# A hybrid decoder layer on one core: the whole up projection in 512-column products, its convolution taps moved from VectorE to ScalarE copies and adding DMAs

## The chip, the cores and the metric

The kernel runs on one core of a Trainium2 chip, in one launch. The metric is the device time of one execution in microseconds (us), the median of several runs. Engines are named as in the profile: PE is TensorE (PEld its weight loads), DVE is VectorE, ACT is ScalarE, POOL is GpSimd and SP is SyncE; POOL and SP issue the DMAs here.

## The reference, cut to what matters

One layer: a token mixer, a layer norm, a gated feed-forward part with a short convolution, and a second layer norm. Everything is float32, SEQ is 512, D_MODEL is 2048 and D_FF is 5632.

```python
def _causal_conv3(x, w):
    xp = jnp.pad(x, ((0, 0), (2, 0), (0, 0)))
    return w[0] * xp[:, :-2] + w[1] * xp[:, 1:-1] + w[2] * xp[:, 2:]

def _conv_ffn(h, w_up, conv_w, conv_b, w_down):
    up = _causal_conv3(h @ w_up, conv_w) + conv_b
    a, g = jnp.split(up, 2, axis=-1)
    return (jax.nn.silu(g) * a) @ w_down

def reference(x, w_in, conv_mix_w, w_out, ln1_g, ln1_b, w_up, ffn_conv_w, ffn_conv_b,
              w_down, ln2_g, ln2_b, rel_bias):
    for layer in range(DEPTH):
        mix = _token_mixer(x, w_in[layer], conv_mix_w[layer], w_out[layer], rel_bias)
        x = _layernorm(ALPHA * x + mix, ln1_g[layer], ln1_b[layer])
        ffn = _conv_ffn(x, w_up[layer], ffn_conv_w[layer], ffn_conv_b[layer], w_down[layer])
        x = _layernorm(ALPHA * x + ffn, ln2_g[layer], ln2_b[layer])
    return x
```

## The kernel before, in words

**Stages.** The input projection (48 pairs of 128-column output tiles), attention with the first part of the output projection, the rest of the output projection with the first layer norm, the up projection (FT = 44 pairs, each one value tile and one gate tile of 128 channels by 512 positions), and the down projection with the second norm. In the trace the up projection lies from about 1245 to 2125 us.

**Precision.** Each float32 operand is split into a rounded high part and a remainder. For weights, ACT writes the high part (`whi`, line 217) and DVE the remainder (`wlo`, line 220); a product is high weight by high activation, high weight by low activation, and low weight by high activation.

**Pairs.** A pair of output tiles is computed by Winograd's form of Strassen's scheme: seven products (numbered 1 to 7 in `PROD`) of quarter blocks. The weight side of a product is a raw block (B11, B21, B22) or one of four sums T1 to T4, which DVE forms into a tile `tt` (line 207). The seven results are combined in PSUM banks, with some partial results copied out by ACT (a "snapshot") before the bank is added to further.

**Narrow and wide products.** In `product` (narrow, lines 372, 373, 376) each of the eight high-weight blocks meets the high and the low activation in two matmuls of 256 columns, and eight more matmuls of 256 columns use the low weight: 24 matmuls. In `product_wide` (lines 349, 352) the high and low activation lie side by side, and one matmul of 512 columns takes both: 16 matmuls. A wide result has two halves in its bank, so a wide pair ends in four combines of two DVE instructions each (an add of bank and snapshot, line 430, and an add of the two halves into the output tile `o`, line 1132), where a narrow pair ends in two (line 670). The input projection's full pairs are all wide. In the up projection, pair 0 is "plain" (ordinary block products), pairs 1 to 5 have products 1 and 2 done ahead and five narrow products left (`MAIN` without 1 and 2), and of pairs 6 to 43 every third is wide (`p % every == 0` with `every` 3): 13 wide, 25 narrow.

**Weights.** Blocks of 1 MB come by SP's queue into `RAWS` = 3 buffers, in order; a load waits until the block three before it has been used up by the last `wlo` that reads it. `pump` runs ahead of PE by RING = 4 operands: when PE is done with an operand, the operand four later gets its sum (DVE), its `whi` (ACT), and the operand before that one its `wlo` (DVE). Each engine executes in program order.

**After a pair.** `done3` is called when all of a pair's output `o` is there. ACT writes `cv` = weight[2] * o + bias (line 1115, two instructions); DVE adds the two shifted taps with `taps` (line 696, two instructions for the gate half, two for the value half), ACT applies Silu to the gate half (line 1119), DVE multiplies (line 1122), and POOL sends 256 KB to `act_d` in DRAM (line 1123). `later(n, fn)` puts a step off by n products: the program emits it after the n-th product from then. The last pair's outputs are read back for the down projection.

## Time and profile before

| | before |
|---|---|
| median of 3 runs | 2617.81 us (2616.57 to 2621.77) |
| the profiled execution, its own time | 2619.59 us |
| its span in the trace | 2617.8 us |
| PE busy | 2586.3 us (99% of the span) |
| DVE busy | 2156.1 us (82%) |
| ACT busy | 1205.6 us (46%) |

The span runs from the first to the last instruction of the trace; the execution's own time is 1.8 us more. Busy time counts every moment in which at least one instruction of the engine is recorded as running; since one instruction's record may reach into the next one's, the mean duration of an instruction can be a little longer than the step from one start to the next.

### The profile page before, as it was taken

How to read it: one execution, taken by the hardware profiler on the slowest of the kernel's cores; microseconds unless marked ns; L12 is line 12 of the kernel's file. 1: busy time of each engine (PE TensorE's matmuls, PEld its weight loads, DVE VectorE, ACT ScalarE, POOL GpSimd, SP SyncE). 2: the span in 40 equal slices, each digit the busy share in tenths (PEclk: the TensorE clock that was granted, in tenths of full speed). 3: DMA queues.
4: the chain of work that ended last, by engine and by line, in shares of the span. 5: the costliest groups of instructions: out<-in, count | busy, mean ns of one | idle time of the engine just before them, and what ended most of it. 6: DMA issues, size and time to landing. Idle time of an engine off the chain costs nothing.

```text
span 2617.8 us, 39148 instructions
## 1 busy us (share of the span) xinstructions
PE 2586.3 (99%) x16034; PEld 2329.8 (89%) x16034; DVE 2156.1 (82%) x2575; ACT 1205.6 (46%) x1617; POOL 125.4 (5%) x217
## 2 busy tenths in 40 slices
PE   8999999999999999999999999999999999999997
PEld 8988888888888878888999999999999988888886
DVE  7999888898898876656899999999999965765557
ACT  5444444444544445434655555555555552222220
POOL 0000100000000002221000000000000000000000
PEclk9999999999999999999999999999999999999999
DMA  7423543433433457643443333333333353434331
GB/s 245 168 102 111 188 150 122 145 137 121 145 137 122 144 200 253 244 177 105 167 159 117 128 110 125 116 123 125 109 129 115 120 205 141 153 125 161 113 129 65
DMA packets 70228, 376.34 MB, mean 144 GB/s; under 512 B 9920, under 2 KB 13792, under 8 KB 35360
## 3 DMA queue, kind: packets, MB, share of 16 engines
q1 hardware_dynamic: 51680, 311.47, 34.0%
q0 software_dynamic: 18368, 62.36, 6.5%
q8 instruction: 126, 2.06, 0.3%
q14 instruction: 54, 0.44, 0.1%
HBM read 328.61 MB, written 48.84 MB: 144 GB/s over the span
## 4 chain that ended last, share of the span: by engine, by line
PE 92%; DVE 4%; DMA 2%; ACT 1%; issue 1%; SPq 0%; POOL 0%; DVEq 0%; ACTq 0%
PE bk L349 27%; PE bk L352 14%; PE bk L376 8%; PE bk L373 8%; PE bk L372 8%; PE bk L517 8%; PE bk L519 8%; PE bk L518 8%; DVE wlo L220 1%; DMA raw<-in_w_in_dram 1%; DVE tt L207 1%; DMA ycr<-yc_d 1%; PE bk L851 1%; PE bk L797 0%; PE bk L781 0%
## 5 line engine op out<-in xcount | busy, mean ns | idle before, releaser
L217 ACT ACTIVATE whi<-raw 128x1024 fp32r<-128x1024 f32 x394 | 413.9, 1057 | 521.2 <-PE bk L519 204.1
L220 DVE TENSOR_TENSOR wlo<-raw,whi 128x1024 fp32r<-128x1024 f32 x394 | 480.0, 1221 | 176.7 <-ACT whi L217 175.9
L217 ACT ACTIVATE whi<-tt 128x1024 fp32r<-128x1024 f32 x360 | 380.6, 1057 | 292.4 <-DVE tt L207 167.6
L220 DVE TENSOR_TENSOR wlo<-tt,whi 128x1024 fp32r<-128x1024 f32 x360 | 439.5, 1221 | 39.6 <-ACT whi L217 36.4
L349 PE MATMUL bk<-S,whi 128*128 128x512 f32 x1760 | 440.9, 392 | 0.0
L349 PEld LDWEIGHTS bk<-S,whi 128*128 128x128 f32 x1760 | 316.5, 189 | 56.9 <-ACT s L449 0.4
L349 PE MATMUL bk<-A,whi 128*128 128x512 f32 x1320 | 330.8, 392 | 0.0
L372 PE MATMUL bk<-S,whi 128*128 128x256 f32 x1152 | 283.1, 283 | 0.8 <-ACT z L470 0.8
L373 PE MATMUL bk<-S,whi 128*128 128x256 f32 x1152 | 282.7, 283 | 0.0
L349 PEld LDWEIGHTS bk<-A,whi 128*128 128x128 f32 x1320 | 237.4, 189 | 44.0 <-ACT whi L217 0.9
L352 PEld LDWEIGHTS bk<-S,wlo 128*128 128x128 f32 x1760 | 240.1, 190 | 17.1
L352 PE MATMUL bk<-S,wlo 128*128 128x256 f32 x1760 | 245.4, 282 | 0.0
L372 PE MATMUL bk<-A,whi 128*128 128x256 f32 x936 | 233.5, 286 | 4.0 <-ACT A L312 2.6
L373 PE MATMUL bk<-A,whi 128*128 128x256 f32 x936 | 232.9, 286 | 1.6 <-DVE A L313 1.5
L372 PEld LDWEIGHTS bk<-S,whi 128*128 128x128 f32 x1152 | 221.1, 192 | 1.7 <-ACT z L470 1.7
L373 PEld LDWEIGHTS bk<-S,whi 128*128 128x128 f32 x1152 | 221.2, 192 | 0.0
L207 DVE TENSOR_TENSOR tt<-raw,tt 128x1024 f32<-128x1024 f32 x180 | 219.2, 1218 | 0.0
L352 PEld LDWEIGHTS bk<-A,wlo 128*128 128x128 f32 x1320 | 180.1, 190 | 12.9
L517 PE MATMUL bk<-whi,A 128*128 128x512 f32 x480 | 186.7, 389 | 0.0
L518 PE MATMUL bk<-wlo,A 128*128 128x512 f32 x480 | 186.7, 389 | 0.0
L519 PE MATMUL bk<-whi,A 128*128 128x512 f32 x480 | 186.7, 389 | 0.0
L372 PEld LDWEIGHTS bk<-A,whi 128*128 128x128 f32 x936 | 181.6, 194 | 5.3 <-ACT A L312 3.1
(206 smaller groups left out, 3985.3 us busy)
## 6 DMA issues: line engine op xcount, KB each, us to landing
raw<-in_w_in_dram SPq DMA_DIRECT2D x97, 1024.0 KB, 4.9
raw<-in_w_up_dram SPq DMA_DIRECT2D x89, 1024.0 KB, 5.3
raw<-in_w_down_dram SPq DMA_DIRECT2D x44, 1024.0 KB, 4.9
qkv_d<-o POOLq DMA_DIRECT2D x36, 512.0 KB, 3.9
raw<-in_w_out_dram SPq DMA_DIRECT2D x16, 1024.0 KB, 6.6
act_d<-z POOLq DMA_DIRECT2D x44, 256.0 KB, 5.2
qk<-qkv_d SPq DMA_DIRECT2D x7, 1536.0 KB, 10.3
ar<-act_d SPq DMA_DIRECT2D x9, 1024.0 KB, 6.9
```

Source lines behind the costliest of these rows:

```text
L207: nc.vector.tensor_sub(self.src, v[0], prev)
L217: nc.scalar.activation(self.hi, self.src, AF.Copy)
L220: nc.vector.tensor_sub(self.lo, self.src, self.hi.bitcast(F32))
L349: mm(ps, op.hi[:, w], X[xn].both(k), start=first and k == 0, stop=False, skip_group_check=True)
L352: mm(ps[:, 256:], op.lo[:, w], X[xn][0][:, k], start=False, stop=last and k == 7, skip_group_check=True)
L372: mm(ps, op.hi[:, w], xh[:, k], start=first and k == 0, stop=False, skip_group_check=True)
L373: mm(ps, op.hi[:, w], xl[:, k], start=False, stop=False, skip_group_check=True)
L376: mm(ps, op.lo[:, w], xh[:, k], start=False, stop=last and k == 7, skip_group_check=True)
L517: mm(banks[n], yh[:, tt], op.hi[:, w], start=first and i == 0, stop=False)
L518: mm(banks[n], yh[:, tt], op.lo[:, w], start=False, stop=False)
L519: mm(banks[n], yl[:, tt], op.hi[:, w], start=False, stop=last and i == 1)
L851: nc.tensor.transpose(ps[:, i * P:(i + 1) * P], src[:, n, s:s + P], ident)
```

## The change: what it does

- **All pairs 6 to 43 of the up projection become wide**: `run_pairs` no longer has `every`.
- **The taps leave DVE**, but for the last pair: in `done3`, ACT copies the pair's output `o` times a tap's weight (into a tile `t` for shift 1, into `o` itself for shift 2; two 512-column instructions for each), and POOL issues a DMA that adds the copy, shifted, to `cv` in SBUF (`accum_op=OP.add`, 512 KB each). The steps are spread over the products that follow: `start` one product later, the taps two and three later, the gate (Silu) nine later (`TAPS`) and the multiply with its store ten later.
- **Weight sums in place of raw blocks**: T1 and T2 overwrite B12, T3 overwrites B11 and T4 overwrites B21. The tiles `tt` go, and `RAWS` becomes 4. T4 now reads B12's place too, so that both blocks of a pair are free only after the pair's last operand. The order of products becomes [1, 5, 2, 6, 3, 7, 4] everywhere (that of `LAST` before), in the input projection too; the scratch tiles that came from `tt` come from the output tiles.
- The stage's small tiles are cut otherwise: `z` from 8 buffers to 4, `cv` two and `t` one of four 256-column blocks.

```diff
+TAPS = 9
-RAWS = 3
+RAWS = 4
-MAIN = [1, 5, 6, 3, 7, 4, 2]
-LAST = [1, 5, 2, 6, 3, 7, 4]
+MAIN = [1, 5, 2, 6, 3, 7, 4]
+REST = [5, 6, 3, 7, 4]
...
-                self.src = tt_tile()
-                prev = v[1] if len(v) > 1 else self.box["T1" if self.kind == "T2" else "T2"]
-                nc.vector.tensor_sub(self.src, v[0], prev)
-                self.box[self.kind] = self.src
+                b = self.box
+                if self.kind == "T1":
+                    b["T"] = v[0]
+                    nc.vector.tensor_sub(b["T"], v[0], v[1])
+                elif self.kind == "T2":
+                    nc.vector.tensor_sub(b["T"], v[0], b["T"])
+                else:
+                    nc.vector.tensor_sub(v[0], v[0], b["T"])
+                self.src = b["T"] if self.kind in ("T1", "T2") else v[0]
...
+            if op.kind == "T2" and ops[i - 1].kind == "T1":
+                back_upto(i)
...
-        parts = {"B11": [b11], "B21": [b21], "B22": [b22], "T1": [b12, b11], "T2": [b22], "T3": [b12, b22],
-                 "T4": [b21]}
+        parts = {"B11": [b11], "B21": [b21], "B22": [b22], "T1": [b12, b11], "T2": [b22, b12], "T3": [b11, b12],
+                 "T4": [b21, b12]}
...
-            seqs.append((p, [q for q in (LAST if p == n - 1 else MAIN) if p >= nplain + npre or q > 2], False))
+            seqs.append((p, MAIN if p >= nplain + npre else REST, False))
...
-            if 1 in seq and put_block and p % every == 0:
+            if 1 in seq and put_block:
                 run_wide(p, seq, X, stile, otile, put_block, done, hook)
...
     def done3(j, o):
-        o = o.rearrange("p (f h) t -> p f (h t)", f=2)
-        cv = [stile3() for _ in range(2)]
-        for f in range(2):
-            ft = j + f * FT
-            nc.scalar.activation(cv[f], o[:, f], AF.Identity, bias=fw_t[:, ft, 3:4], scale=fw_t[:, ft, 2:3])
+        def fh(t):
+            return t.rearrange("p (f h) t -> p f (h t)", f=2)
+
+        o, cv, last = fh(o), fh(cvtile()), j == FT - 1
+
+        def start():
+            for f in range(2):
+                ft = j + f * FT
+                nc.scalar.activation(cv[:, f], o[:, f], AF.Identity, bias=fw_t[:, ft, 3:4], scale=fw_t[:, ft, 2:3])
+
+        def tap(sh):
+            t = fh(cvtile("t", 1)) if sh == 1 else o
+            for f in range(2):
+                ft = j + f * FT
+                nc.scalar.activation(t[:, f], o[:, f], AF.Copy, scale=fw_t[:, ft, 2 - sh:3 - sh])
+            nc.gpsimd.dma_start(cv[:, :, sh:], t[:, :, :S - sh], accum_op=OP.add)
 
         def gate():
-            taps(cv[1], o[:, 1], fw_t[:, j + FT])
-            nc.scalar.activation(cv[1], cv[1], AF.Silu)
+            if last:
+                taps(cv[:, 1], o[:, 1], fw_t[:, j + FT])
+            nc.scalar.activation(cv[:, 1], cv[:, 1], AF.Silu)
...
-        later(1, gate)
-        later(2, lambda: taps(cv[0], o[:, 0], fw_t[:, j]))
-        later(3, mul)
+        if last:
+            start()
+            later(1, gate)
+            later(2, mul)
+            return
+        later(1, start)
+        for sh in (1, 2):
+            later(1 + sh, functools.partial(tap, sh))
+        later(TAPS, gate)
+        later(TAPS + 1, mul)
...
-    run_pairs(plan3, X, stile3, otile3, bands, done3, act_first, block3, 3)
+    run_pairs(plan3, X, stile3, otile3, bands, done3, act_first, block3)
```

DVE in the middle of the up projection, before: the end of one wide pair and the beginning of a narrow one (`raw` are weight blocks, `tt` the sums, `z` snapshots and convolution tiles, `o` the output tile, `bk` a bank).

```order
L430 TENSOR_TENSOR z_16735<-bk_2537_16876,z_16735 128x512
L1132 TENSOR_TENSOR o_16848<-z_16735 128x256
L207 TENSOR_TENSOR tt_16967<-raw_16773,tt_16868 128x1024
L220 TENSOR_TENSOR wlo_16932<-tt_16929,whi_16931 128x1024
L696 SCALAR_TENSOR_TENSOR z_16938<-o_16848,fw_t,z_16938 128x511
L696 SCALAR_TENSOR_TENSOR z_16938<-o_16848,fw_t,z_16938 128x510
L220 TENSOR_TENSOR wlo_16970<-tt_16967,whi_16969 128x1024
L696 SCALAR_TENSOR_TENSOR z_16937<-o_16848,fw_t,z_16937 128x511
L696 SCALAR_TENSOR_TENSOR z_16937<-o_16848,fw_t,z_16937 128x510
L220 TENSOR_TENSOR wlo_17004<-raw_16773,whi_17003 128x1024
L1122 TENSOR_TENSOR z_16937<-z_16937,z_16938 128x512
```

DVE at the like place of the change, from the last combine of one pair to the first of the next:

```order
L436 TENSOR_TENSOR z_16311<-bk_2325_16264,z_16311 128x512
L1164 TENSOR_TENSOR o_16218<-z_16311 128x256
L211 TENSOR_TENSOR raw_16027<-raw_16027 128x1024
L224 TENSOR_TENSOR wlo_16308<-raw_16029,whi_16307 128x1024
L211 TENSOR_TENSOR raw_16029<-raw_16029,raw_16027 128x1024
L224 TENSOR_TENSOR wlo_16337<-raw_16027,whi_16336 128x1024
L224 TENSOR_TENSOR wlo_16361<-raw_16029,whi_16360 128x1024
L1147 TENSOR_TENSOR cv_16133<-cv_16133 128x512
L436 TENSOR_TENSOR z_16305<-bk_2338_16342,z_16305 128x512
L1164 TENSOR_TENSOR o_16400<-z_16305 128x256
L207 TENSOR_TENSOR raw_16209<-raw_16209 128x1024
L224 TENSOR_TENSOR wlo_16388<-raw_16209,whi_16387 128x1024
```

The four tap instructions (L696) are gone, the multiply (now L1147) belongs to the pair before the one that has just ended, and each pair has four such combines.

ACT over the same stretch of the change, from the copy for a pair's last combine (L433) over the snapshots (L455), `start` (L1130), the gate (L1142) and the tap copies (L1136) to the next pair's operands (L221):

```order
L433 ACTIVATE z_14855<-bk_2085_14650 128x512
L455 ACTIVATE z_14877<-bk_2118_14860 128x512
L221 ACTIVATE whi_14880<-raw_14571 128x1024
L1130 ACTIVATE cv_14859<-o_14762,fw_t 128x512 x2
L221 ACTIVATE whi_14904<-raw_14573 128x1024
L1142 ACTIVATE cv_14677<-cv_14677 128x512
L1136 ACTIVATE t_14909<-o_14762,fw_t 128x512 x2
L455 ACTIVATE z_14929<-bk_2112_14832 128x512
L221 ACTIVATE whi_14931<-raw_14753 128x1024
L1136 ACTIVATE o_14762<-o_14762,fw_t 128x512 x2
L221 ACTIVATE whi_14964<-raw_14753 128x1024
L221 ACTIVATE whi_14984<-raw_14755 128x1024
```

Before, the same place held the two instructions of line 1115 and one Silu among the seven conversions; four scaled copies have come in, and the gate is that of the pair before (cv_14677, where `start` writes cv_14859).

POOL's queue in the same stretch of the change; before, a pair had one row of it, the store to `act_d`:

```order
L1137 DMA cv_14677<-o_14580 128x2x510
L1137 DMA cv_14859<-t_14909 128x2x511
L1148 DMA act_d<-cv_14677 128x512
L1137 DMA cv_14859<-o_14762 128x2x510
L1137 DMA cv_15041<-t_15091 128x2x511
L1148 DMA act_d<-cv_14859 128x512
```

Between a pair's two adding DMAs now stands the store of the pair before.

## Rows read from the trace of the kernel before

**Rows 1.** The page's first part and the chain of work that ended last, by engine: busy us, share of the span, instructions; then shares of the span.

```profile
PE 2586.3 (99%) x16034; PEld 2329.8 (89%) x16034; DVE 2156.1 (82%) x2575; ACT 1205.6 (46%) x1617; POOL 125.4 (5%) x217
...
PE 92%; DVE 4%; DMA 2%; ACT 1%; issue 1%; SPq 0%; POOL 0%; DVEq 0%; ACTq 0%
```

**Rows 2.** Busy time of each engine (and instructions) in stretches of 100 us; the first two lie in the input projection where all pairs are wide, the others in the up projection. After the engines: TensorE's granted clock, DMA share, GB/s.

```profile
600.00:700.00 100.00, 100.00 (x575) 88.02 (x574) 87.46 (x97) 49.13 (x58) 3.58 (x5) 1.00 0.38 137
700.00:800.00 100.00, 100.00 (x576) 88.02 (x575) 90.12 (x97) 48.73 (x57) 3.57 (x5) 1.00 0.37 132
...
1300.00:1400.00 100.00, 99.15 (x769) 96.00 (x769) 98.91 (x111) 58.20 (x81) 3.25 (x6) 1.00 0.38 132
1400.00:1500.00 100.00, 100.00 (x749) 95.97 (x748) 92.42 (x100) 53.91 (x70) 3.24 (x6) 1.00 0.36 121
```

**Rows 3.** PE's timeline in a narrow pair: start us, us, the low-weight group of eight that ends each product.

```profile
1696.59 1.12 PE L376 MATMUL bk<-S,wlo 128*128 128x256 f32 x8
1699.47 1.12 PE L376 MATMUL bk<-S,wlo 128*128 128x256 f32 x8
1702.35 1.12 PE L376 MATMUL bk<-A,wlo 128*128 128x256 f32 x8
```

**Rows 4.** The same in a wide pair: the 512-column group of eight that begins each product.

```profile
1731.93 2.00 PE L349 MATMUL bk<-S,whi 128*128 128x512 f32 x8
...
1734.73 2.00 PE L349 MATMUL bk<-S,whi 128*128 128x512 f32 x8
...
1737.52 2.00 PE L349 MATMUL bk<-S,whi 128*128 128x512 f32 x8
```

**Rows 5.** Groups by line from 1320 to 2100 us on ACT: form, count, busy us, mean ns of one, idle time before them and what ended it.

```profile
L217 ACT ACTIVATE whi<-tt 128x1024 fp32r<-128x1024 f32 x159 | 167.7, 1055 | 89.8 <-DVE tt L207 61.3 <-PE bk L349 20.9 <-PE bk L373 7.7
...
L1115 ACT ACTIVATE z<-o,fw_t 128x512 f32<-128x512 f32 x80 | 60.6, 805 | 14.0 <-DVE o L1132 11.8 <-DVE o L670 2.2
...
L1119 ACT ACTIVATE z<-z 128x512 f32<-128x512 f32 x40 | 25.3, 633 | 20.9 <-DVE z L696 20.9
L449 ACT ACTIVATE z<-bk 128x512 f32<-128x512 f32 x39 | 23.1, 592 | 37.2 <-PE bk L352 37.2
```

**Rows 6.** DVE's timeline through that wide pair: start us, us.

```profile
1732.33 1.54 DVE L696 SCALAR_TENSOR_TENSOR z<-o,fw_t,z 128x511 f32<-128x511 f32 x2 [0.18 <-ACT z L1115]
1733.78 1.22 DVE L220 TENSOR_TENSOR wlo<-tt,whi 128x1024 fp32r<-128x1024 f32 x1
...
1737.65 0.68 DVE L1122 TENSOR_TENSOR z<-z,z 128x512 f32<-128x512 f32 x1
1738.25 1.22 DVE L207 TENSOR_TENSOR tt<-raw 128x1024 f32<-128x1024 f32 x1
...
1741.59 1.22 DVE L207 TENSOR_TENSOR tt<-raw,tt 128x1024 f32<-128x1024 f32 x1
1742.72 1.22 DVE L220 TENSOR_TENSOR wlo<-tt,whi 128x1024 fp32r<-128x1024 f32 x1
1743.86 0.68 DVE L430 TENSOR_TENSOR z<-bk,z 128x512 f32<-128x512 f32 x1
1744.57 0.43 DVE L1132 TENSOR_TENSOR o<-z 128x256 f32<-128x256 f32 x1
1744.92 1.22 DVE L220 TENSOR_TENSOR wlo<-tt,whi 128x1024 fp32r<-128x1024 f32 x1
```

**Rows 7.** The only copies of ACT with a scale from a tile in this kernel (the mixer's convolution): min/median/max ns, first and last start, form.

```profile
L708 ACT ACTIVATE o<-o,cw_t x8: 707/716/726, 86.8 to 245.1; 128x512 f32<-128x512 f32 x8
```

**Rows 8.** DMA issues by line: tile, queue, count, KB each, median us from issue to landing; and the spread of the stores to `act_d` and of their read-back.

```profile
raw<-in_w_up_dram SPq DMA_DIRECT2D x89, 1024.0 KB, 5.3
act_d<-z POOLq DMA_DIRECT2D x44, 256.0 KB, 5.2
yc_d<-o POOLq DMA_DIRECT2D x4, 512.0 KB, 3.0
ycr<-yc_d POOLq DMA_DIRECT2D x1, 1024.0 KB, 17.1
...
DMA to landing us min/median/max: 2.3/5.2/14.2
```

**Rows 9.** The entry of the up projection: waits from 1200 to 1270 us (us, times, longest); the chain there; a stretch of 20 us behind it.

```profile
ACT whi L217 <- DMA raw<-in_w_up_dram: 2.7, 1, 2.7
...
PE bk L1035 <- ACT S L1039: 1.8, 1, 1.8
...
1245.30 5.03 DMA raw<-in_w_up_dram
1250.42 1.06 ACT whi L217
...
1262.70:1282.70 20.00, 19.93 (x161) 19.73 (x160) 19.35 (x26) 14.81 (x26) 0.00 (x0) 0.95 0.44 158
```

**Rows 10.** The start of the kernel: the chain, and busy time in stretches of 5 us.

```profile
28.22 4.65 DMA raw<-in_w_in_dram
32.98 1.06 ACT whi L217
...
30.00:35.00 5.00, 2.39 (x9) 1.72 (x9) 4.04 (x6) 3.43 (x6) 0.00 (x0) 0.75 0.94 287
35.00:40.00 5.00, 4.86 (x25) 4.67 (x25) 4.50 (x7) 3.45 (x5) 0.00 (x0) 0.57 0.87 299
```

More of the change, by code (lines that the diff above doesn't have):

```diff
@@ L183, in load_next @@
         st["load"] += 1
-    def tt_tile():
-        return wpool.tile([P, UNIT], F32, tag="tt", name=nm("tt"), bufs=3)
     class Op:
@@ L457, in run_wide, with run_pairs @@
                 hook(p, q)
-    def run_pairs(pl, X, stile, otile, bands, done, hook=None, put_block=None, every=1):
+    def run_pairs(pl, X, stile, otile, bands, done, hook=None, put_block=None):
         for p, seq, pre in pl:
@@ L540, in s_alloc, with s_first @@
         X["pools"] = pools
-    def s_first(X, raw, k):
+    def s_first(X, raw, k, scratch):
         ks = slice(k, k + 2)
         a11, a21, a22 = raw["S2"][k // 2][:, 0], raw["S4"][k // 2][:, 0], raw["S4"][k // 2][:, 1]
-        s3 = tt_tile().rearrange("p (s t) -> p s t", t=256)[:, :2]
+        s3 = scratch()[:, :2]
         put(X, "A22", ks, a22)
@@ L582, in layer_kernel, with otile1 @@
     tp = mkpool(tps, "tp1", "right")
+    def otile1():
+        return tp.tile([P, 4, 256], F32, tag="o", name=nm("o"), bufs=3)
     def x_load(i, k):
@@ L589, in x_split @@
         split(X[n][0][:, k:k + 2], X[n][1][:, k:k + 2], raw["S2"][k // 2][:, i])
-    wt = tt_tile()[:, :256 + P]
+    wt = otile1().rearrange("p a t -> p (a t)")[:, :256 + P]
     nc.vector.memset(wt, 0.0)
@@ L624, in layer_kernel @@
         plan_work(XS + i // 2, x_split, 1, 2 * i)
-        plan_work(XF[i], s_first, X, raw, 2 * i)
-        plan_work(XR[i], s_rest, X, raw, 2 * i)
+        plan_work(XF[i], s_first, X, raw, 2 * i, otile1)
+        plan_work(XR[i], s_rest, X, raw, 2 * i, otile1)
     hook = schedule(todo)
@@ L949, in otile3, with cvtile @@
         return chp.tile([P, 4, 256], F32, tag="o", name=nm("o"), bufs=2)
+    def cvtile(tag="cv", bufs=2):
+        return chp.tile([P, 4, 256], F32, tag=tag, name=nm(tag), bufs=bufs)
     def keep3():
@@ L954, in stile3, with ztiles @@
     def stile3(b=None):
-        return zbp.tile([P, 512], F32, tag="z", name=nm("z"), bufs=8)
-    def ztile(t):
-        return stile3() if t >= 2 else zap.tile([P, 512], F32, tag="z", name=nm("z"), bufs=8)
-    z = [[ztile(t) for c in range(4)] for t in range(4)]
+        return zbp.tile([P, 512], F32, tag="z", name=nm("z"), bufs=4)
+    def ztiles(t):
+        if t == 2:
+            return [o.rearrange("p (a b) t -> p a (b t)", a=2)[:, i] for o in (cvtile(), cvtile()) for i in range(2)]
+        return [stile3() if t == 3 else zap.tile([P, 512], F32, tag="z", name=nm("z"), bufs=8) for c in range(4)]
+    z = [ztiles(t) for t in range(4)]
     for c in range(4):
@@ L1076, in layer_kernel @@
         plan_work(HF + 2 * i + 1, tr_k, 2 * i + 1, 1, raw["S4"])
-        plan_work(HF + 2 * i + 1, s_first, X, raw, 2 * i)
-        plan_work(HR[i], s_rest, X, raw, 2 * i)
+        plan_work(HF + 2 * i + 1, s_first, X, raw, 2 * i, otile3)
+        plan_work(HR[i], s_rest, X, raw, 2 * i, otile3)
     hook = schedule(todo)
@@ L1110, in done3 @@
     def done3(j, o):
-        o = o.rearrange("p (f h) t -> p f (h t)", f=2)
-        cv = [stile3() for _ in range(2)]
-        for f in range(2):
-            ft = j + f * FT
-            nc.scalar.activation(cv[f], o[:, f], AF.Identity, bias=fw_t[:, ft, 3:4], scale=fw_t[:, ft, 2:3])
+        def fh(t):
[11 more added lines that the diff above has]
+            nc.gpsimd.dma_start(cv[:, :, sh:], t[:, :, :S - sh], accum_op=OP.add)
         def gate():
-            taps(cv[1], o[:, 1], fw_t[:, j + FT])
-            nc.scalar.activation(cv[1], cv[1], AF.Silu)
+            if last:
+                taps(cv[:, 1], o[:, 1], fw_t[:, j + FT])
+            nc.scalar.activation(cv[:, 1], cv[:, 1], AF.Silu)
         def mul():
-            nc.vector.tensor_mul(cv[0], cv[0], cv[1])
-            nc.gpsimd.dma_start(act_d[:, j, :], cv[0])
-        later(1, gate)
-        later(2, lambda: taps(cv[0], o[:, 0], fw_t[:, j]))
-        later(3, mul)
+            if last:
+                taps(cv[:, 0], o[:, 0], fw_t[:, j])
+            nc.vector.tensor_mul(cv[:, 0], cv[:, 0], cv[:, 1])
+            nc.gpsimd.dma_start(act_d[:, j, :], cv[:, 0])
+        if last:
+            start()
[7 more added lines that the diff above has]
+        later(TAPS + 1, mul)
     run_plain(plan3, X, otile3, done3, hook)
```

7 lines of the change are left out of this document (2 added, 5 removed).

## The prediction, made before the changed kernel had run

> **What bounds the kernel now.** I read the page's first part and its chain first: PE is busy 99% of the span and holds 92% of the chain that ended last [rows 1], so time is saved only where PE gets less to do, or where one of its few stalls goes. The stretches come next: in the up projection PE is at 99 to 100% at a granted clock of 1.00, with DVE at 92 to 99% and ACT at 54 to 58% [rows 2]. So PE sets the pace there and DVE is the engine nearest to taking over. In the stretch at 98.9% DVE, PE was still at 99.15%: the four operands that run ahead of PE hide a DVE that is almost full. Last I read the timelines of a narrow and a wide pair, for the step from one product to the next.
>
> **What PE saves.** The low-weight groups of a narrow pair start at 1696.59, 1699.47 and 1702.35, 2.88 us apart [rows 3]. The 512-column groups of a wide pair start at 1731.93, 1734.73 and 1737.52, on average 2.795 apart [rows 4]. Both forms stream the same columns; the wide one has eight instructions fewer. The change turns 25 pairs of seven products from narrow to wide: 175 products by 0.085 us are 14.9 us. Pair 0, the five pairs with five products each and the products done ahead stay narrow, and the input projection was wide already; their new order alone moves nothing on PE. The clock is at 1.00 on both sides.
>
> **What DVE pays and gets back.** Of a wide pair the starts [rows 6] give 1.14 us for a 1024-column instruction (1741.59, 1742.72, 1743.86), 1.06 for a combine of two (1743.86 to 1744.92), 1.45 for two taps (1732.33 to 1733.78) and 0.60 for the multiply (1737.65 to 1738.25). A pair has seven remainders and four sums, eleven by 1.14, or 12.5 us; with four combines, 4.2, and the multiply, 0.6, that is 17.4. PE needs 7 x 2.795 = 19.57. With its taps a wide pair takes 20.3, more than PE: now every third pair overruns and the narrow ones between make it good. Without taps all of them fit, with 2.2 us to spare. Sums written in place are as many and as long as before. The input projection is a trial of such a load: wide pairs, DVE 87 to 90%, PE 100% [rows 2].
>
> **What ACT takes on.** Per pair: seven conversions at 1.06, four bank copies at 0.59, `start` at 2 x 0.76, a Silu of 0.63 [rows 5], and four scaled copies at 0.72 [rows 7]: 7.4 + 2.4 + 1.5 + 0.6 + 2.9 = 14.8 of 19.57 us, so ACT has room on average. But they come bunched. From the end of the sum T4 on, ACT's order is the rest of `start` (about 0.1), whi of T4, Silu, two copies, snapshot, whi, two copies, whi of the next T1: 0.1 + 1.06 + 0.63 + 1.43 + 0.59 + 1.06 + 1.43 + 1.06 = 7.4 us. DVE in that time has two remainders, the multiply, one combine, a sum and a remainder (4 x 1.14 + 0.6 + 1.06 = 6.2), then waits for the conversion of T1: 1.2 us a pair. 17.4 + 1.2 = 18.6 still lies under 19.57. The bounds: no wait, where ACT starts ahead of DVE, or all 3.5 us by which the inserted Silu and copies could hold it up. I take 1.2, hidden under PE's 19.57. If that cover were gone, 38 pairs would each pay what lies above, less once about 5 us that the four operands ahead absorb (three products of 2.8 less one conversion and one remainder, with queueing).
>
> **The adding DMAs.** The trace has none. They hang together as a circle: Silu of one pair stands ahead of the tap copies of the next on ACT and waits for its second DMA; that waits on POOL for the first to land; the first waits for its copies. Per pair, then, 0.63 + 1.43 + D1 + D2, with D the time from issue to landing; it stays hidden while D1 + D2 is below 19.57 - 2.06 = 17.5 us. From below D is 3.0 us, the plain 512 KB store; from above 17.1, a 1,024 KB load by POOL among others in flight [rows 8]. An addition has to read its target too, so the nearest row is the 1,024 KB weight load, 5.3. I take 5.3 for the second, and 8 for the first, since both 1 MB loads of a pair are now released together just before it and share the engines: 13.3, four under the limit. The store of the pair before stands between the two on POOL, behind a multiply that comes no later than the first DMA lands; the weight loads themselves now have a whole pair's time to land.
>
> The Trainium skill (Collectives: The Full Stack, section The bandwidth ceiling) says that an addition in the DMA path is slow for its two source reads, not for the adding; by that a 512 KB adding DMA is a 1,024 KB one on the read side, and the sum of this part would come out the same. No row here shows it.
>
> **Small terms.** Entry of the up projection: a load issued at 1245.30 holds a conversion up by 2.7 us, on the chain; PE then stands 1.8 us for ACT, and the clock over the next 20 us is 0.95, some 1 us [rows 9]. With four buffers that load leaves one block earlier. Between 0 and 2.8; I take 2.0 off. Start: one load on the chain (28.22, 4.65 us) precedes a stretch with PE busy 2.39 of 5 us and the clock at 0.75 and 0.57 [rows 10]. The fourth buffer brings that load forward, but the second half of x's blocks still waits behind the next one, and the DMA engines are 94% busy. Between 4 less and 1 more; I take 1.0 off. Pairs 1 to 5: only five products apart, so `start` of pair p + 2 comes one product after the multiply of pair p and needs its buffer, which is free when the store has landed, 5.2 us [rows 8]. ACT stands there some 3 us in each of four pairs of 14.4; between 0 and 3 us reach PE; I take 1.0 on.
>
> **Sum.** 14.9 + 2.0 + 1.0 - 1.0 = 16.9 off the profiled execution's 2619.6 (span 2617.8) gives 2602.7; the median of the runs lies 1.8 lower, so 2601 is forecast. With the bounds of the small terms together the likeliest case runs from 2596 to 2607.
>
> **Rivals.**
> - *The adding DMAs land late* (slower). For: the first shares the engines with 2 MB of weights, rows are offset by one or two elements, and landing spreads from 2.3 to 14.2 us for a mere 256 KB [rows 8]. Against: the rows nearest to it leave four us. The place is the gate at nine products, where ACT stands and the next conversions behind it, then DVE's remainders, then PE. From 17.5 on each us costs 38 us less the 5 once; the gain of 17 is used up at 18.1. At 19.5 (2 us a pair) the time is 2601 + 76 - 5 = 2672. 0.13.
> - *DVE becomes the bound through ACT's bunches.* If the wait is 2.8 instead of 1.2, a pair takes 20.2: 38 x 0.63 - 5 = 19 more, 2620, no change. For: 1.2 rests on every hand-over in its turn, and snapshots also wait for PE. Against: now ACT's conversions of sums stand idle for 89.8 us in 780, waiting for DVE and PE [rows 5], and DVE ran at 99% without loss to PE [rows 2]. 0.13, of which 0.03 ends above 2623.
> - *The stalls at start and entry vanish wholly, clock and all*: 2.8 + 4 instead of 3, 2594 to 2596 and a little below. 0.04.
> - *The forecast*, 2596 to 2607: 0.70.
>
> **Chances.** A measurement of this kernel can tell about 0.2%, 5.2 us. Faster than 2612.6: 0.70 + 0.04 and a little of the second rival, 0.76. Within: 0.09. Slower than 2623: 0.12 + 0.03, 0.15. The range reaches from 2594 to 2625, into the second rival, and leaves out about 0.16, nearly all of it late DMAs.
>
> **What would show it.** Right: in the up projection 16 matmuls a product, steps of 2.795, PE at 100%, DVE near 90%, ACT near 76%, and Silu's idle time small. The adding DMAs land in 4 to 9 us; if the idle time before Silu grows towards microseconds a pair and ends on the landing in `cv`, the first rival holds. If instead DVE's idle time before its remainders, ended by ACT's conversions, nears 2.2 us a pair and PE waits for DVE, the second does. The wait for the weight load at the entry should be gone, and PE's stall behind it smaller. I am wrong most of all if an adding DMA costs much more than a plain one of twice its bytes.

## The result, and the profile after

The changed kernel takes 2631.1 us (median of 4 runs, 2629.4 to 2634.5) where the kernel before, run beside it, takes 2618.8. The ratio is 1.0048, with a 95% interval of 1.0035 to 1.0060: slower by 12.3 us, where 2601 was forecast. The profiled execution took 2629.4 us, with a span of 2626.9; it is the fastest of the four, and lies 9.8 us above the profiled execution of the kernel before.

The page's first part after, which answers to [rows 1], and busy time by stretches of the up projection, which answers to [rows 2] (columns as there):

```profile
PE 2580.1 (98%) x14634; PEld 2264.0 (86%) x14634; DVE 2108.7 (80%) x2553; ACT 1318.0 (50%) x1789; POOL 229.2 (9%) x303
```

```profile
1300.00:1400.00 100.00, 87.13 (x606) 83.19 (x606) 68.23 (x69) 58.04 (x85) 14.91 (x16) 0.91 0.67 174
1400.00:1500.00 100.00, 100.00 (x574) 87.99 (x573) 87.39 (x100) 68.61 (x93) 15.92 (x17) 1.00 0.68 174
1600.00:1700.00 100.00, 100.00 (x575) 88.08 (x574) 89.55 (x103) 68.64 (x92) 14.77 (x15) 1.00 0.68 173
...
2100.00:2200.00 100.00, 89.95 (x412) 74.58 (x411) 49.90 (x57) 42.41 (x57) 8.53 (x12) 0.95 0.62 203
```

The 1400 instructions fewer on PE are there (16034 to 14634), and from 1400 to 2100 us the stage is what was forecast: PE at 100.00, DVE at 87 to 90 where it was at 91 to 93, ACT at 68 to 69. The first and the last stretch are not: at 1300 PE has 87.13 of 100 us and a mean clock of 0.91, at 2100 it has 89.95 and 0.95. Before, PE had 99.15 in the first of these [rows 2], and 100.00 in the last. PE's timeline in a wide pair, as in [rows 4]:

```profile
1501.05 2.00 PE L355 MATMUL bk<-A,whi 128*128 128x512 f32 x8
...
1503.84 2.00 PE L355 MATMUL bk<-S,whi 128*128 128x512 f32 x8
...
1506.64 1.55 PE L355 MATMUL bk<-S,whi 128*128 128x512 f32 x6
```

The steps are 2.79 and 2.80 us. The DMA issues by line, as in [rows 8], are where something new shows:

```profile
raw<-in_w_up_dram SPq DMA_DIRECT2D x89, 1024.0 KB, 7.4
...
cv<-t POOLq DMA_DIRECT2D x43, 511.0 KB, 9.5
cv<-o POOLq DMA_DIRECT2D x43, 510.0 KB, 5.0
...
act_d<-cv POOLq DMA_DIRECT2D x44, 256.0 KB, 9.5
...
ar<-act_d POOLq DMA_DIRECT2D x2, 1024.0 KB, 11.7
```

The two adding DMAs land after 9.5 and 5.0 us, 14.5 together, under the limit of 17.5. The store to `act_d`, which the change hardly touches, went from 5.2 to 9.5.

Where the difference lies is read from the starts of certain matmuls in the trace of both kernels (us; the third column is the best kernel found below):

| start of | before | after | best |
|---|---|---|---|
| first product of the attention's output projection | 973.8 | 969.9 | 972.3 |
| first transpose ahead of the up projection | 1209.0 | 1203.8 | 1206.2 |
| first wide product of the up projection | 1367.1 | 1370.6 | 1363.2 |
| first product of the down projection | 2125.3 | 2127.1 | 2106.2 |
| last product | 2603.8 | 2613.3 | 2585.8 |

At the first transpose the changed kernel is 5.1 us ahead. It loses 8.6 us in the next stage, which holds pairs 1 to 5 (the short pairs, of five products each); gains only 1.7 us in the stage of the wide pairs, where 14.9 were due; and loses 7.6 us behind the entry of the down projection, a stage whose code is untouched. These stages cut across the two losses that follow: the last stall of the first one (1384 us) already lies among the wide pairs, and the second begins at the end of their stage.

**The first loss: the pairs of five products.** Waits from 1295 to 1400 us (us in total, times, longest); then POOL's and ACT's timelines, and the chain, at the first of these waits:

```profile
ACT cv L1130 <- DMA act_d<-cv: 22.4, 4, 7.5
...
PE bk L378 <- ACT z L476: 8.1, 3, 5.2
```

```profile
1318.21 1.19 POOL L1137 DMA_DIRECT2D cv<-o  x1 [4.46 <-ACT z L476]
1318.96 1.02 POOL L1148 DMA_DIRECT2D act_d<-cv  x1
```

```profile
1329.90 1.52 ACT L1130 ACTIVATE cv<-o,fw_t 128x512 f32<-128x512 f32 x2 [7.46 <-DMA act_d<-cv]
```

```profile
1318.96 10.85 DMA act_d<-cv
...
1330.62 0.80 ACT cv L1130
...
1340.22 9.27 DMA act_d<-cv
...
1360.19 9.62 DMA act_d<-cv
```

The store stands on POOL 0.75 us behind the second adding DMA of the next pair and lands 10.85 us after its issue. `start` of pair p + 2 (L1130) needs that buffer of `cv` and waits for it in place on ACT, 7.46 us, with the conversions behind it; four such waits are 22.4 us. PE, which is ahead by some products, loses 0.6, 5.4, 2.6 and 5.0 us in its turn, at 1317, 1332, 1355 and 1384 us, 13.5 in all. At the end of each of the last three, while PE still stands, the granted clock falls to its lower level, 1.2 GHz. A stretch at the first of them:

```profile
1335.00:1345.00 10.00, 7.18 (x38) 7.18 (x39) 7.69 (x9) 5.31 (x9) 1.84 (x3) 0.66 0.83 195
```

In the trace that level lasts 6.8, 3.4 and 6.8 us, 17.1 in all; PE works in 14.8 of them and loses half of that, 7.4 us. Together with the stalls that is some 21 us.

The second adding DMA, too, is late here. Of the transfers `cv<-o` from 1300 to 1385 us:

```profile
DMA to landing us min/median/max: 5.1/9.7/10.5
```

The prediction took 5.3 for it, and the wide pairs show 5.0 (5.0 to 6.4 from 1400 to 2100 us). In the trace no weight load is in flight beside it there; in the short pairs one or two are, in four cases of five, and the first adding DMA, which has them beside it in the wide pairs (9.6 us), lands in 5.1.

**The second loss: the entry of the down projection.** POOL's timeline, then the chain:

```profile
2114.52 1.19 POOL L1137 DMA_DIRECT2D cv<-t  x1 [8.35 <-ACT t L1136]
2115.24 1.61 POOL L1113 DMA_DIRECT2D ar<-act_d  x2
```

```profile
2115.24 10.75 DMA ar<-act_d
2126.01 1.07 ACT A L318
2127.09 0.98 DVE A L319
```

The read-back of the first rows of `act_d` (two transfers of 1 MB), which the down projection needs as its first operand, stands on POOL behind the first adding DMA of pair 42, the last but one. That one is only issued when ACT has made its copies, at 2114.52. The first half of the read-back lands 10.75 us after its issue, and PE, done with the up projection at 2121.3, stalls for 5.95, 3.3 and, later, 1.7 us, with 10.2 us at the lower clock. In the kernel before it was issued 3.6 us earlier, and PE came to the down projection only at 2125.3:

```profile
2111.60 1.07 POOL L1103 DMA_DIRECT2D ar<-act_d  x2 [13.19 <-ACT z L470]
```

### The profile page after: what moved, and what is told of

It is laid out like the page before. It is cut to its first block, busy times and chain, and to the rows that moved or that the text cites. A ratio compares the mean times of both kernels' runs of the same rounds, so it can differ in the third digit from the quotient of the medians.

```text
span 2626.9 us, 36631 instructions
## 1 busy us (share of the span) xinstructions
PE 2580.1 (98%) x14634; PEld 2264.0 (86%) x14634; DVE 2108.7 (80%) x2553; ACT 1318.0 (50%) x1789; POOL 229.2 (9%) x303
## 4 chain that ended last, share of the span: by engine, by line
PE 44%; DMA 3%; DVE 2%; ACT 1%; issue 0%; POOL 0%; DVEq 0%; ACTq 0%; POOLq 0%; SPq 0%
PE bk L355 18%; PE bk L358 9%; PE bk L524 6%; PE bk L525 5%; PE bk L523 5%; DMA act_d<-cv 1%; DMA ar<-act_d 1%; DMA cv<-t 0%; DVE zz L1246 0%; ACT whi L221 0%; DVE zz L1248 0%; DVE bst L1030 0%; ACT t L1136 0%; DVE zz L1027 0%; ACT cv L1130 0%
## 5 line engine op out<-in xcount | busy, mean ns | idle before, releaser
L221 ACT ACTIVATE whi<-raw 128x1024 fp32r<-128x1024 f32 x754 | 790.9, 1055 | 838.9 <-PE bk L525 202.3
L224 DVE TENSOR_TENSOR wlo<-raw,whi 128x1024 fp32r<-128x1024 f32 x754 | 919.2, 1221 | 187.0 <-ACT whi L221 172.8
L355 PE MATMUL bk<-S,whi 128*128 128x512 f32 x2560 | 643.1, 393 | 5.0 <-ACT z L455 4.8
L355 PEld LDWEIGHTS bk<-S,whi 128*128 128x128 f32 x2560 | 461.5, 189 | 88.0 <-ACT z L455 5.0
L355 PE MATMUL bk<-A,whi 128*128 128x512 f32 x1920 | 481.2, 392 | 0.0
L358 PEld LDWEIGHTS bk<-S,wlo 128*128 128x128 f32 x2560 | 350.1, 191 | 25.1
L358 PE MATMUL bk<-S,wlo 128*128 128x256 f32 x2560 | 357.8, 283 | 0.0
L358 PEld LDWEIGHTS bk<-A,wlo 128*128 128x128 f32 x1920 | 261.9, 190 | 18.7
L358 PE MATMUL bk<-A,wlo 128*128 128x256 f32 x1920 | 267.7, 282 | 0.0
L455 ACT ACTIVATE s<-bk 128x512 f32<-128x512 f32 x126 | 75.2, 597 | 128.8 <-PE bk L358 128.7
L455 ACT ACTIVATE z<-bk 128x512 f32<-128x512 f32 x114 | 67.3, 591 | 92.7 <-PE bk L358 92.7
L209 DVE TENSOR_TENSOR raw<-raw,raw 128x1024 f32<-128x1024 f32 x90 | 109.7, 1219 | 0.4
L211 DVE TENSOR_TENSOR raw<-raw 128x1024 f32<-128x1024 f32 x90 | 109.8, 1220 | 0.0
L211 DVE TENSOR_TENSOR raw<-raw,raw 128x1024 f32<-128x1024 f32 x90 | 109.7, 1219 | 0.0
```

What stands on the lines that cost most here:

```text
L209: nc.vector.tensor_sub(b["T"], v[0], b["T"])
L211: nc.vector.tensor_sub(v[0], v[0], b["T"])
L221: nc.scalar.activation(self.hi, self.src, AF.Copy)
L224: nc.vector.tensor_sub(self.lo, self.src, self.hi.bitcast(F32))
L355: mm(ps, op.hi[:, w], X[xn].both(k), start=first and k == 0, stop=False, skip_group_check=True)
L358: mm(ps[:, 256:], op.lo[:, w], X[xn][0][:, k], start=False, stop=last and k == 7, skip_group_check=True)
```

## The experiments

All are edits of the changed kernel. Times are medians beside runs of the kernel before on the same chip (2618 to 2619 us).

**1. An earlier gate in the pairs of five products.**

```
-        later(TAPS, gate)
-        later(TAPS + 1, mul)
+        wait = 6 if j < 6 else TAPS
+        later(wait, gate)
+        later(wait + 1, mul)
```

> The gate of pairs 0 to 5 comes six products after their output instead of nine, the multiply and store seven; all else is the changed kernel. Theory: between 1315 and 1395 us of the changed kernel ACT stood at `start` for the store that frees `cv` (22.4 us in four waits, each store 9 to 11 us to landing, one product after the multiply); PE lost 13.5 us and 17.1 us at half clock, 8.5 us more. With four products of 2.88 us between multiply and `start` the store has landed: the waits at `start` fall under 3 us in all, the stretch has no stall over 1 us and a clock of 1.00, and the time is 18 to 22 us below the changed kernel. Rival (these short pairs have too much work for ACT and the adding DMAs in 14.4 us each, whatever is waited for): the wait only moves to Silu, which stands for its adding DMAs, and the time falls by less than 8 us.

Measured: 2641.0 us, 1.0081 [1.0064, 1.0098], some 10 us slower still. Waits from 1295 to 1430 us:

```profile
DVE cv L1147 <- ACT cv L1142: 28.4, 6, 8.8
ACT cv L1142 <- DMA cv<-o: 28.4, 5, 9.4
```

ACT's wait for the store is gone, and a longer one stands in its place: Silu (L1142) now waits for the second adding DMA, as the rival had it, and the time rose instead of falling a little. First adding DMA, second adding DMA and store land one after the other, with ACT's copies between them; moving the gate only changed which of them ACT stands for. So this place for the gate was no cure, and the expectation failed; other places were not tried.

**2. The additions left out.**

```
-            nc.gpsimd.dma_start(cv[:, :, sh:], t[:, :, :S - sh], accum_op=OP.add)
+            nc.gpsimd.dma_start(cv[:, :, sh:], t[:, :, :S - sh])
```

> The taps' DMAs copy instead of adding, so the convolution keeps one tap alone of three; sizes, places and order are those of the changed kernel. If the addition is what makes these DMAs long (each reads its target too): the first falls from a median of 9.5 us to 5 to 7, the second from 5.0 to about 3.5, the store behind it from 9.5 to 5 to 7, the wait at `start` in the short pairs from 22.4 us to under 12, and the time by 5 to 12 us. If sharing the engines with the two weight loads is what does it: all three stay within 1 us of where they are.

Measured: 2608.8 us in one execution. DMA issues, and the stretch of the short pairs:

```profile
cv<-t POOLq DMA_DIRECT2D x43, 511.0 KB, 8.1
cv<-o POOLq DMA_DIRECT2D x43, 510.0 KB, 3.1
act_d<-cv POOLq DMA_DIRECT2D x44, 256.0 KB, 8.0
```

```profile
1300.00:1400.00 100.00, 99.51 (x718) 94.08 (x717) 84.45 (x89) 71.79 (x103) 12.26 (x19) 1.00 0.58 211
```

These medians are those of the wide pairs. There the addition costs 1.9 us where no weight load is in flight (5.0 against 3.1) and 1.4 in the first DMA; most of the first one's 9.5 us, and of the store's, is there for plain copies too. In the short pairs more goes: `cv<-o` from 1300 to 1385 us, where the changed kernel has 5.1/9.7/10.5, shows

```profile
DMA to landing us min/median/max: 3.1/3.3/3.4
```

and the store behind it 5.1 to 5.3 in place of 9.3 to 10.85 at the three longest waits. ACT's waits at `start` shrink from 22.4 to 6.6 us, and the short pairs' stalls are gone but for 0.6 us: PE 99.51 and a clock of 1.00. The time fell by 22 us, not by 5 to 12, and the first DMA and the store stayed longer than expected, so neither case came as written. The Trainium skill (Collectives: The Full Stack, section The bandwidth ceiling), drawn on in the prediction, has the adding step of a collective slow for its two source reads; the 5.0 us of the 510 KB adding DMA, against 3.1 for the plain copy and 5.0 for a 1,024 KB load of the input projection, agree with that, though no run here separates the reads from the adding.

**3. A third buffer for `cv`.** It needs 4 KB a partition, and the room comes from the fourth weight buffer, of 8 KB; the first run below is its base, the second has the buffer too. Both have the read-back moved, as in experiment 4.

```
-RAWS = 4
+RAWS = 3
...
-        if q == 2:
+        if q == 5:
```

> The changed kernel with the read-back three products later, and three weight buffers of 8 KB instead of four: the base for the next run, which needs the room. If the fourth buffer is needed by sums that stay in their blocks until the last of them is converted: 2625 to 2650 us, with ScalarE's conversions or VectorE's sums waiting for weight loads from 1400 us on. If a pair's time is enough for the loads anyway: 2619.5 us, as with four.

Measured: 2624.9 us, 1.0020 [1.0011, 1.0029]. From 1400 to 2100 us PE is busy 700.00 of 700 us with three buffers as well, so the in-place sums of the wide pairs don't need the fourth there; the 5.4 us against the same kernel with four lie elsewhere (a stall of 4.9 us at 964.7 instead of 1.57; and from the first transpose to the first wide product 170.9 us instead of 166.6, with two more stalls at the entry of the up projection). The time is at the edge of the first case, but not by what that case supposed.

```
-    def cvtile(tag="cv", bufs=2):
+    def cvtile(tag="cv", bufs=3):
```

> As the run with three weight buffers, and a third buffer for cv in the room that is freed; all taps stay spread, in the pairs of five products too. Theory (what stalls pairs 1 to 5 is that the start of a pair needs the buffer whose store landed 10 us after issue; with a third it needs a store one pair of 14.4 us older): the 22 us between 1317 and 1395 us go, that is 18 to 22 us less than the run with three weight buffers and two of cv; ScalarE's waits for act_d there under 1 us. Rival (the adding DMAs themselves are too slow for 14.4 us a pair, 14.5 us for the two and some 2 for the copies): the wait moves to Silu or to the copies, and no more than 10 us come back.

Measured: 2604.3 us, 0.9944 [0.9931, 0.9958], 20.5 us less than its base. ACT's timeline at the start of a short pair, and the stores' landing from 1300 to 1400 us:

```profile
1329.20 1.05 ACT L221 ACTIVATE whi<-raw 128x1024 fp32r<-128x1024 f32 x1
1330.15 1.51 ACT L1130 ACTIVATE cv<-o,fw_t 128x512 f32<-128x512 f32 x2
1332.89 1.06 ACT L221 ACTIVATE whi<-raw 128x1024 fp32r<-128x1024 f32 x1 [1.22 <-DVE raw L209]
```

```profile
DMA to landing us min/median/max: 5.0/9.0/11.1
```

`start` follows the conversion without a wait, while the stores land as late as before (9.0 us, up to 11.1). So neither ACT nor the adding DMAs were too slow for pairs of 14.4 us: the reuse of the second buffer was what tied them together. Some 19 to 20 us come back when the short pairs do without these transfers (experiment 6) and when the transfers stay as late and have a buffer more, so the first loss is settled.

**4. The read-back one product earlier.** The edit of `act_first` shown above alone, with four weight buffers. In the pairs' order of products 5 stands ahead of 2, so the read-back is issued one product earlier, ahead of the last first-tap DMA; where the expectations of other runs here say "three products later, behind the last adding DMA", that is wrong, and this order is meant.

> The read-back of the first eight blocks of `act_d` is issued after the last pair's product 5, one product earlier, and so ahead of pair 42's first adding DMA; all else is the changed kernel. Theory: it starts 2.8 to 4 us earlier and lands before the adding DMA has taken its share: PE's stall at 2121 us shrinks from 9.3 to under 4 us, the time falls by 6 to 13 us. Rival (conversions on ACT are the limit there): the load lands earlier, but PE's stall stays above 6 us.

Measured: 2619.5 us, 1.0000 [0.9991, 1.0010], 11.6 less than the changed kernel. POOL's timeline, and the stretch at the entry of the down projection:

```profile
2105.62 1.17 POOL L1113 DMA_DIRECT2D ar<-act_d  x2 [1.87 <-PE bk L358]
2112.48 1.23 POOL L1137 DMA_DIRECT2D cv<-t  x1 [5.69 <-ACT t L1136]
```

```profile
2100.00:2200.00 100.00, 98.47 (x459) 82.07 (x458) 59.52 (x68) 47.24 (x62) 9.16 (x13) 1.00 0.63 210
```

The read-back goes ahead of the adding DMA, 9.6 us earlier where 2.8 to 4 were expected, its first half lands 5.6 us after its issue instead of 10.75, and PE's loss shrinks to a stall of 1.7 us. So the late read-back is the second loss. How much of the cure is the earlier issue and how much the shorter landing was not told apart.

**5. The taps of the last two pairs on VectorE**, the read-back where the change has it:

```
-        o, cv, last = fh(o), fh(cvtile()), j == FT - 1
+        o, cv, last = fh(o), fh(cvtile()), j >= FT - 2
```

> The last two pairs, not the last one alone, get their taps on DVE; so no adding DMA is issued within the last pair's products. Theory: the stall of PE at 2121 us of the changed kernel (9.3 us in two pieces, 1.7 at 2171, clock 0.5 for 10.2 us) comes of the read-back of `act_d`, which POOL issues behind pair 42's first adding DMA and which lands 10.8 us later. Without that DMA the read-back is issued some 3 us earlier and lands in 6 to 9 us: the stall shrinks to under 4 us and the time falls by 8 to 14 us. Rival (the last pair has too many conversions on ACT, with four of the read-back among them): ACT's order is the same, and with four more taps DVE is fuller; the time falls by less than 4 us or rises.

Measured: 2625.9 us, 1.0028 [1.0017, 1.0038]; but the stall at the entry of the down projection stays, 6.5 us and 3.3. POOL's timeline:

```profile
2114.01 0.62 POOL L1148 DMA_DIRECT2D act_d<-cv  x1 [9.98 <-DVE cv L1147]
2114.62 1.10 POOL L1113 DMA_DIRECT2D ar<-act_d  x2
```

No adding DMA is near, yet the read-back is issued as late: now it stands behind the store of pair 42, which waits for DVE's multiply. So its place in POOL's order counts, not the kind of DMA that stands ahead of it: POOL comes to it only when the step ahead has been released. Its landing is no wait for that DMA: the store lands 2.9 us after its issue, and the read-back's first half still takes 9.6, with two weight loads of the down projection in flight. In the profiled execution the 5 us show as the later stall of 1.7 us, which is gone, and as 6.8 us less at the lower clock (at most 3.4 us of time) in the short pairs, which the edit doesn't touch; the latter is no gain of this edit.

**6. The taps of the short pairs on VectorE, alone and with 4.**

```
-        o, cv, last = fh(o), fh(cvtile()), j == FT - 1
+        o, cv, last = fh(o), fh(cvtile()), j < 6 or j == FT - 1
```

> Pairs 0 to 5 keep their taps on VectorE and start at once, as in the kernel before; the rest is the changed kernel (late read-back too). Theory (the stalls between 1317 and 1395 us come from the chain of two adding DMAs and the store behind them, which five products a pair do not cover): the 13.9 us of stalls and the 8.5 us that 17 us at half clock cost go, less about 2 us of stalls that remain; 2611 us (2608 to 2614). The read-back's stall near 2121 us stays at about 6 us. Rival (those stalls come from the weight loads or the sums of the short pairs, not from the taps): 2631 us, stalls there as in the changed kernel.

> Both cures together: taps of pairs 0 to 5 on VectorE, and the read-back of the first two quarters of act issued three products later, behind the last adding DMA. Theory: the two losses are independent and add up: 2631.1 - 20 - 11.6 = 2599.5 us (2597 to 2603), which is what was predicted for the change itself (2601). Rival (a stall cured in one place comes back in the other): between 2604 and 2611 us.

Measured: 2612.5 us, 0.9979 [0.9969, 0.9989], and with the earlier read-back 2602.5 us, 0.9941 [0.9926, 0.9956]. The first loss is therefore worth 18.7 us, and the two together 28.6 of the 30.3 that they are worth apart. The first stretch of the latter, and the wide pairs:

```profile
1300.00:1400.00 100.00, 97.88 (x708) 92.39 (x707) 97.76 (x108) 57.48 (x80) 4.48 (x7) 1.00 0.41 143
...
1400.00:2100.00 700.00, 700.00 (x4010) 616.22 (x4010) 622.93 (x714) 481.17 (x647) 107.53 (x110) 1.00 0.69 177
```

**7. All taps on VectorE**, all pairs wide (`last` true for every pair), read-back as in 4: what the spread copies and adding DMAs are worth.

> All pairs in 512-column form, but all taps on VectorE and no adding DMA; read-back three products later. Theory of the prediction: VectorE then needs 20.3 us in a pair of 19.57 us, so each of 38 wide pairs pays 0.73 us, less some 5 us once: 23 us more than the kernel with both cures, 2622 us (2616 to 2628), VectorE at 100% from 1400 to 2100 us and TensorE below 100%. Rival (VectorE's 20.3 is overstated, or the overrun is absorbed): 2600 us, and then the adding DMAs and spread copies bring nothing.

Measured: 2636.2 us, 1.0070 [1.0055, 1.0085], 33.7 more than with the taps spread in the wide pairs. DVE, busy 98%, is the bound; the stretch, and PE's timeline at a pair's end:

```profile
1400.00:2100.00 700.00, 675.19 (x3821) 588.61 (x3820) 687.25 (x817) 376.76 (x477) 18.37 (x34) 1.00 0.32 115
```

```profile
1600.14 2.11 PE L355 MATMUL bk<-S,whi 128*128 128x512 f32 x8 [0.74 <-ACT z L455]
```

Once a pair PE stands still for about 0.9 us; the pairs come 20.56 us apart (the product behind such a stall starts at 1600.14 and at 1620.70), which is 1.0 above 19.57 where 0.73 was expected. From the first wide product to the down projection the kernel takes 778.6 us, against 743.0 with the taps spread. The expected 20.3 was the sum of DVE's work without the 2% in which DVE waits for others.

**8. The other half of the change alone**: in-place sums, four weight buffers, the new order, but every third pair alone wide and all taps on VectorE; then the same with the read-back as in 4.

```
-    run_pairs(plan3, X, stile3, otile3, bands, done3, act_first, block3)
+    run_pairs(plan3, X, stile3, otile3, bands, done3, act_first, block3, 3)
```

> The other half of the change alone: sums in place of raw blocks, the four weight buffers, the pools and the order of products as in the changed kernel; but every third pair alone in 512-column form, and all taps on VectorE, as in the kernel before. Theory (this half moved the stalls at the start, before the attention's output projection and at the entry of the up projection): 2618.8 + 2.4 - 7.5 - 2 = 2612 us (2609 to 2616). Rival (in-place sums bring nothing once the taps are as before): 2619 us.

> As the kernel of sums alone (every third pair wide, all taps on VectorE), but the read-back is issued three products later. In the run of the sums alone the read-back was issued at 2115.22 us, directly behind the store of the pair before, and TensorE lost 10.5 us in stalls and 5.1 us to half clock there. Theory (that loss is the place of the read-back in the queue of GpSimd, also without any adding DMA, and the sums themselves gain some 6 us over the kernel before): 2626.0 - 14 = 2612 us (2609 to 2615). Rival (the loss belongs to the sums or to the four buffers, not to that place): 2622 to 2626 us.

Measured: 2626.0 us, 1.0033 [1.0021, 1.0044], which neither theory had; and 2614.7 us, 0.9986 [0.9976, 0.9995]. POOL's timeline in the former:

```profile
2114.69 0.54 POOL L1148 DMA_DIRECT2D act_d<-cv  x1 [21.29 <-PE bk L382]
2115.22 1.07 POOL L1113 DMA_DIRECT2D ar<-act_d  x2
```

As in experiment 5 the read-back stands behind a store, since these taps are done with both halves in two steps instead of three and the multiply comes a product earlier than in the kernel before. That store lands 3.2 us after its issue, the read-back's first half 10.7 after its own. With the read-back moved, as the theory of the second run had it (2609 to 2615), the sums, the new order and the fourth buffer are worth some 4 us by themselves.

**9. Both cures, and the last two pairs' taps on VectorE** (`j < 6 or j >= FT - 2`, and the earlier read-back).

> The kernel with both cures, and the taps of the last two pairs instead of the last one on VectorE. Theory: the stall of 1.75 us near 2142 us, where the down projection waits for the read-back of the last rows of act, goes, as it did when this was done alone; the rest is as before: 2602.5 - 2 = 2600.5 us. Rival (pair 14 then crowds VectorE in the last pairs): 2602 to 2606 us.

Measured: 2600.7 us, 0.9929 [0.9917, 0.9942]: the lowest median here, 18 us under the kernel before and 30 under the change as it was made, though the 1.8 us below experiment 6 with 4 are not clear of noise. The stall of 1.75 us near 2142 is gone; one of 0.9 us is left, at 2106. The pair that the expectation calls 14 is pair 42.

## Why the prediction was wrong

**PE's saving was right.** Steps of 2.79 and 2.80; from the first wide product to the down projection the best kernel takes 743.0 us against 758.2 before, 15.2 less where 14.9 were worked out.

**DVE and ACT in the wide pairs were right.** DVE 87 to 90%, PE 100%, no sign of the second rival: DVE's waits for ACT stay inside PE's 19.57 us. ACT shows 69%, not the 76% of the sum, because durations of single instructions overlap by some 0.1 us in the rows, which the sum left in for ACT and took out for DVE. That such pairs can't keep their taps on DVE was right in kind, and the price was higher than the rows gave (33.7 us, experiment 7).

**The adding DMAs in the wide pairs were nearly right**: 9.5 and 5.0 where 8 and 5.3 were taken, 14.5 for 13.3, under the 17.5. The first rival, as stated, didn't happen: past 1400 us nothing waits for them on the path of PE.

**The step that failed first is the small term on pairs 1 to 5.** The mechanism was named: `start` of pair p + 2 waits for the store of pair p, five products apart. Its price was 1.0 us, at most 3, from a store that lands in 5.2 us. It cost 18.7 us (experiment 6). Two things were left out. The store's 5.2 us was taken over from a kernel in which it shares the engines with one weight load; behind an adding DMA, with weight loads beside both, it takes 9.5, and up to 10.85 in the short pairs. The second adding DMA, taken at 5.3, takes 7.9 to 10.5 there in four of five. And each stall of PE was costed by its length alone, while the granted clock fell with it, which [rows 9, 10] had shown twice. The limit of 17.5 us for the adding DMAs is worked out for pairs of seven products; in pairs of five the same sum leaves 14.4 - 2.06 = 12.3, less than the prediction's own 13.3. That was never worked out, though the text says that these pairs are only five products apart. It would not have been the right mechanism (with a third buffer the short pairs run freely), but it would have shown that they had no margin.

**The second step that failed was missing.** The end of the stage was not priced: the read-back of `act_d` stands on POOL among the new DMAs, and no term asks what is queued there behind an adding DMA that waits for ACT's copies. Nor does one ask when PE, faster by the saving, needs it. It cost 11.6 us (experiment 4), or 10.0 with the short pairs cured.

**Start and entry.** The entry's gap is 1.73 us instead of 2.0, and the half clock behind it is gone (2.0 was taken; from the first transpose to the first wide product experiment 6 with 4 takes 157.0 us instead of 158.1). At the start 1.0 was taken off and 2.4 us came on: the first attention matmul begins at 966.25 instead of 963.86. Of that 1.4 us are a new stall right in front of it, for DVE's last work on the input projection:

```profile
966.25 1.79 PE L786 MATMUL bk<-qk 128*128 128x128 f32 x8 [1.41 <-DVE su L436]
```

A stall near 70 us is new too; it is 1 to 4 us long in all of these kernels with four buffers. Not priced at all was a gain of 7.5 us from there to the first transpose. The load that PE waited for, `ycr` [rows 8], now lands sooner:

```profile
ycr<-yc_d POOLq DMA_DIRECT2D x1, 1024.0 KB, 12.4
```

Before, PE stood 6.65 us for it; now PE comes 2.4 us later, the load is there 3.9 us earlier, and 0.5 us of waiting is left. So the loss at the start is contained in this gain, and the two together are the 5.1 us at the first transpose. The fourth buffer is not what brings the load forward: with three it lands after 12.1 and 12.4 us as well (experiment 3). What does stays open. With three buffers PE stands 4.9 to 5.3 us at another place, in front of the attention's first matmul, while ACT waits for a weight load of the output projection.

**The rest of the sum.** The third rival's 2594 to 2596 doesn't follow from its terms: 2.8 + 4 in place of 3 is 3.8 off 2601, or 2597. Without the two failed steps experiments 6 with 4 and 9 measure 2602.5 and 2600.7 us, against the 2601 forecast. Part of that closeness is luck. In the trace of experiment 6 with 4 the wide pairs bring 15.2 us for 14.9 and the entry 1.2 for 2.0; but up to the first transpose 4.7 come off where 1.0 was taken for another reason, and the down projection takes 480.6 us instead of 478.5, which no term has.

## What to carry to other kernels

Before a step is moved onto a DMA, check its latency in the shortest iteration of the loop, not in the usual one, and count every buffer that waits for it: here two buffers held for wide pairs and not for short ones. Take the landing time of a transfer from a row in which the same transfers are in flight with it, and go through the issuing engine's order at each change of stage. Where latency doesn't fit only a few iterations, leave those on the old path: that alone brought back 19 of 30 us.

## What the runs showed of the hardware

**How late a transfer lands goes with what is in flight beside it, from either queue.** The 256 KB store on POOL's queue took 2.3 us with nothing in flight, 5.2 beside one weight load (kernel before), 5.0 right behind an adding DMA without a weight load, and 9.5 behind an adding DMA with one or two weight loads in flight; behind a plain copy of 511 KB with these loads it still took 8.0 (experiment 2). The adding DMA itself took 5.0 us without a weight load beside it (4.95 to 6.4 in 40 cases of the changed kernel) and 9.6 (median) with one or two, whichever of a pair's two it was. The first half of the 2 MB read-back took 9.6 to 12.0 us in the six kernels in which weight loads of the down projection were in flight at its issue, behind an adding DMA, a plain copy or a store that itself landed in 3 us; 7.2 us in the kernel before, with such a load in flight and nothing else; and 4.9 to 5.9 us where no weight load was in flight at its issue, in five of these seven kernels though an adding DMA was. The weight loads from SP's queue grew too, 5.3 to 7.4 us, at a DMA share of 0.68 instead of about 0.36. The Trainium skill says (DMA: Bandwidth & Descriptors, section Issuing engines are not separate DMA queues) that transfers of all issuing engines run on the same 16 DMA engines and interleave; the longer weight loads beside POOL's new transfers agree.

**Stalls cost more than their length.** With PE's stalls of 2.6 to 6 us in the short pairs and at the down projection of the changed kernel the granted clock fell to 1.2 GHz, for 3.4 to 10.2 us; the stall of 1.7 us at 2171 went without that. It fell while PE still stood: at 1336.97 in the stall that ended at 1337.82, at 2125.45 in the one that ended at 2127.12. Only what PE does in that time costs: 14.8 of 17.1 us in the short pairs and, with the second stall inside, 5.8 of 10.2 at the down projection, half of which, 7.4 and 2.9 us, is lost. The stalls of 5.95 and 3.3 us and these 2.9 make 12.2 us, which is near the 11.6 of experiment 4. The second stretch:

```profile
2120.00:2136.00 16.00, 7.48 (x24) 5.63 (x23) 8.87 (x9) 6.74 (x7) 1.22 (x1) 0.68 0.76 224
```
